# Wide gate-weight splits on VectorE, squares of the last norms in PSUM, and output additions held behind the splits

## The chip, the cores and the metric

The kernel runs on one core of a Trainium2 chip. The metric is the device time of one execution in microseconds (us). The core's engines work side by side, each through a queue of its own in order: TensorE (PE: matmuls, and PEld: weight loads), VectorE (DVE), ScalarE (ACT), GpSimd (POOL), and SyncE (SP), which issues most DMAs. One instruction that waits holds up all that stands behind it on its engine.

## The reference, cut to what matters

One layer of a streaming encoder: token mixers, a gated MLP, then a gated per-layer input. The change touches its end, from the MLP's last down-projection on:

```python
f = (gelu(f_gate) * f_val) @ w_ffn_down        # 2816 -> 1024
h = h + rmsnorm(f, g_ffn_post)                  # second residual
e = p @ w_ple_proj
g = sigmoid(h @ w_ple_gate)                     # the gate, 1024 -> 1024
h = h + rmsnorm(e * g, g_ple_post)              # output
```

There are 1024 tokens and 1024 features, all in float32.

## The kernel before

Activations are held transposed: a tile is 128 features by 1024 tokens, and the work goes in two halves of 512 tokens (half 0 and half 1). A float32 matmul is made of three in a rounded format: each operand is split into `hi`, a rounded copy, and `lo`, the rest, and `linear` adds hi·hi, lo·hi and hi·lo into one PSUM bank. `split` is therefore everywhere: ACT writes `hi` with a CAST (L182), then DVE or POOL writes `lo = src - hi` (L183).

SBUF is cut into 51 slots of 128x1024, PSUM is one tile of eight 128x512 banks. The Python code gives data dependencies; the order of the instructions on each engine is made by a scheduler with a timeline of its own, which may move an instruction far ahead of its place in the code. `tc.issue_after(x)` keeps what it wraps behind the instruction x.

The end of the kernel is written as follows. `down_tail(fX, h)` makes the last six of 22 slices of the down-projection: for each of eight output tiles 18 matmuls, then on DVE `y += psum` (in `down`, L953; half 1 only). `second_residual(h)` squares the eight tiles of y on ACT (`square_sum`, L250), adds the squares up on DVE (L253), and calls `rstd`: matmuls with ones (L230), a short chain on DVE and ACT (L234 to L240, the root on ACT needs a table load), and transposes that spread the result over a PSUM bank (L242). Then for each of eight tiles k: y times the norm (L1037, DVE, reads PSUM), h = d_h1 + y (L1038; POOL for odd k, DVE for even k; `d_h1` is loaded into one of four half slots, so that the loads for k = 4 to 7 wait for the splits of k = 0 to 3), and the split of h (cast on ACT, `lo` on DVE for odd k, on POOL for even k).

The gate follows: `load_all` loads the eight 512 KB weight tiles and splits each in two blocks of 512 columns (`block`: cast on ACT, `lo` on POOL). The loop runs over three pieces (half 0; half 1 in two pieces of 256 tokens). For each of eight tiles of a piece: 24 matmuls (L217), the sigmoid on ACT (L1060, another table than the root's), times e on DVE (L1061), and the square (L250) and its addition (L253). Then `rstd`, and per tile k `hi + lo` on POOL (L1068, it gives h back), the norm on DVE (L1069), their sum (L1070) and the DMA to `out` (L1071).

The squares of these last norms lie in SBUF slots: `sqs` and `sqs2` are rings of half tiles.

Of the kernel before, what the change touches and what calls it, by code (L numbers as in the profile page):

```python
# [28 lines left out]
NBLK = 7  # L29
# [48 lines left out]
def kernel(  # L78
# [19 lines left out]
    nc = tc.nc  # L98
    V, G, A = nc.vector, nc.gpsimd, nc.scalar
# [14 lines left out]
    def slot(i, dt):  # L114
        b, j = quad_of.get(i, (i, None))
        if held[b][0] != dt:
            n = S if j is None else 4 * S
            held[b] = (dt, apool.tile([P, n], dt, tag=f"s{b}", name=f"s{b}"))
        t = held[b][1]
        return t if j is None else t[:, j * S : (j + 1) * S]  # L120
# [8 lines left out]
    def f32(i):  # L129
        return slot(i, F32)  # L130

    def f32r(i):
        return slot(i, F32R)

    def hs(h):
        return slice(h * HALF, (h + 1) * HALF)

    def single(i, h):
        return f32(i)[:, hs(h)]

    def singles(*slots):

        return [(i, h) for i in slots for h in range(2)]
# [5 lines left out]
    def f(ap):  # L149
        return ap.bitcast(F32)  # L150

    def bank(i, n=1):
        return psum[:, i * HALF : (i + n) * HALF]
# [7 lines left out]
    def col(name, i=0):  # L161
        c = COL[name] + i
        return vecs[:, c : c + 1]
# [14 lines left out]
    wblk = Ring(range(NBLK))  # L178
    last = []

    def split(src, hi, lo, eng=None):
        A.copy(hi, src)  # L182
        last.append((eng or V).tensor_sub(lo, src, f(hi)))  # L183
        return last[-1]

    def block(src, eng=None, dst=None):

        n = src.shape[1]
        hi, lo = parts(wblk() if dst is None else dst)
        split(src, hi[:, :n], lo[:, :n], eng or G)  # L190
        return hi, lo

    def wide(src, eng):

        hi, lo = f32r(wblk()), f32r(wblk())
        split(src, hi, lo, eng)
        return [(hi[:, hs(i)], lo[:, hs(i)]) for i in range(2)]

    def load_w(src, raws, cols=1024, dst=(None, None), eng=None):

        raw = f32(raws())
        nc.sync.dma_start(raw[:, :cols], src)
        return [block(raw[:, c : min(c + HALF, cols)], eng, d) for c, d in zip(range(0, cols, HALF), dst)]

    def load_all(w, raws, others):

        where = [None] * NBLK + list(others)
        return [load_w(w[c], raws, dst=where[2 * c : 2 * c + 2]) for c in range(8)]

    def linear(out_ps, w, wc, X, half, cs=None, start=True, stop=True):  # L210

# [33 lines left out]
    def square_sum(acc, src, accs, sqs):  # L245

        n = src.shape[1]
        at = (accs if acc is None else sqs)()
        sq = (single(*at) if isinstance(at, tuple) else bank(at))[:, :n]
        A.activation(sq, src, AF.Square)  # L250
        if acc is None:
            return sq
        V.tensor_add(acc, acc, sq)  # L253
        return acc
# [129 lines left out]
    raws = Ring([7, 8, 42, 43])  # L384
    mm = Ring(range(6))
# [39 lines left out]
    sqs, accs = Ring(singles(44)), Ring(singles(45))  # L425
    es = Ring(range(29, 33))
    B, first, second, third = x_blocks(u, [*range(9, 33), *range(38, 42)])
    for h in range(2):
        acc = None
        for k in range(8):  # L430
            acc = square_sum(acc, single(u[k], h), accs, sqs)
# [36 lines left out]
    w = gate_weights(spilled, True)  # L468
    third(w)
    others = Ring([44, 46])  # L470
# [84 lines left out]
    for grp, dim, pairs in (("kv", 256, ((3, 4),)), ("q", 384, ((0, 1), (2, 5)))):  # L555
        acc = [None, None]
# [33 lines left out]
    raws = Ring([7, 8])  # L590
# [105 lines left out]
    for k in (3, 4):  # L696
# [3 lines left out]
    extra = {  # L700
        2: lambda: [latent(k, "q", "g_q_lat", k) for k in range(3)],
        4: rotary_key,
        13: lambda: key(0, 0, mm),
        14: lambda: [query(0, h, mm) for h in range(2)],
    }
# [25 lines left out]
    sbk, tpb, pob = Ring(range(4)), Ring([4, 5, 6]), Ring([7])  # L731
# [98 lines left out]
    mm = Ring(range(4))  # L830
    mg = Ring(range(42, 51))
    for ft in range(8):
        if ft % 2 == 0:
            w = load_w(w_bout[ft // 2], raws)
# [15 lines left out]
    sqs, accs, accs2 = Ring([5, 6]), Ring(singles(47)), Ring(singles(49))  # L850
    xrs = Ring(singles(42, 43))
    sbk, rbk = Ring([4]), Ring([7])
    B, first, second, third = x_blocks(u, [*range(9, 33), *range(38, 42)])
    for h in range(2):
        acc = None
        for ft in range(8):
# [3 lines left out]
            acc = square_sum(acc, pt, accs, sqs)  # L860
        R = rstd(acc, D, sbk(), rbk())
        acc = None
        for k in range(8):
# [6 lines left out]
            acc = square_sum(acc, y, accs2, sqs)  # L870
# [24 lines left out]
    raws = Ring([42, 43, 7, 8])  # L895
    mm = Ring(range(4))
# [4 lines left out]
    w = up_weights(order[0])  # L901
# [30 lines left out]
    extra = [i for i in free if i not in quad_of][:2]  # L932
    free = [i for i in free if i not in extra]
    yacc = [*free[:6], *before[1:]]
    extra = [42, 43, *extra]
# [55 lines left out]
    mm = Ring(range(6))  # L991
    ends = {}
    for g in range(2):
# [3 lines left out]
        raws = Ring([7, 8] if g else [7, 8, 45, 50])  # L997
# [7 lines left out]
        w = down_weights(0)  # L1005
# [3 lines left out]
        raws = Ring([10, 11, 7, 8] if g else [45, 50, 7, 8])  # L1009
        for i in range(4):  # L1010
            if i:
                w = down_weights(i)
# [7 lines left out]


    hrs = Ring(singles(12, 9))
    sqs, sqs2, accs = Ring(singles(extra[2])), Ring(singles(extra[3])), Ring(singles(50))
    hX = [[None, None] for _ in range(8)]
    hslots = [*range(29, 33), *range(13, 17)], range(17, 25)
    SS, RB = 6, 7

    def second_residual(h):
        acc = None
        for k in range(8):  # L1030
            acc = square_sum(acc, single(yacc[k], h), accs, sqs)
        R = rstd(acc, D, SS, RB)
        for k in range(8):
            hr = single(*hrs())
            nc.sync.dma_start(hr, d_h1[k, :, hs(h)])
            y = single(yacc[k], h)
            V.scalar_tensor_tensor(y, y, col("g_ffn_post", k), R, op0=ALU.mult, op1=ALU.mult)  # L1037
            (G if k % 2 else V).tensor_add(hr, hr, y)  # L1038
            hX[k][h] = parts(hslots[h][k])
            split(hr, *hX[k][h], V if k % 2 else G)  # L1040

    second_residual(0)
    down_tail(fX, 1)
    second_residual(1)

    mm = Ring(range(4))
    sbk, rbk = Ring([4, 5, 6]), Ring([7])
    ers, ors = Ring(singles(10, 11)), Ring(singles(42, 12, 9, 7, 8))
    wgs = load_all(w_gate, raws, [*range(25, 29), 43, *range(38, 42)])
    for h, o, n in ((0, 0, 512), (1, 0, 256), (1, 256, 256)):  # L1050
        acc = None
        cs = slice(o, o + n)
        base = h * HALF + o
        for ft in range(8):
            er = single(*ers())[:, :n]
            nc.sync.dma_start(er, d_e[ft, :, base : base + n])
            pt = bank(mm())[:, :n]
            linear(pt, wgs[ft], 0, hX, h, cs)
            g_ = single(yacc[ft], h)[:, cs]
            A.activation(g_, pt, AF.Sigmoid)  # L1060
            V.tensor_mul(g_, g_, er)  # L1061
            acc = square_sum(acc, g_, accs, sqs2)
        R = rstd(acc, D, sbk(), rbk(), n)
        for k in range(8):
            o_ = single(*ors())[:, :n]
            g_ = single(yacc[k], h)[:, cs]
            hi, lo = hX[k][h]
            G.tensor_add(o_, f(hi[:, cs]), f(lo[:, cs]))  # L1068
            V.scalar_tensor_tensor(g_, g_, col("g_ple_post", k), R, op0=ALU.mult, op1=ALU.mult)  # L1069
            (G if k in (0, 2, 4) else V).tensor_add(o_, o_, g_)  # L1070
            (nc.sync if k % 2 else A).dma_start(out[k * P : (k + 1) * P, base : base + n], o_)  # L1071
# [101 lines left out]
```

## Time and profile before

| | us |
|---|---|
| median of 3 runs | 1529.71 |
| lowest and highest of them | 1528.55, 1529.9 |
| the profiled execution's time | 1530.54 |
| its span, first to last instruction | 1528.7 |
| PE busy | 1472.8 (96%) |
| DVE busy | 1179.2 (77%) |
| ACT busy | 698.6 (46%) |
| POOL busy | 524.0 (34%) |
| mean granted TensorE clock | 0.987 |

PE is busy nearly throughout, so what can be won lies in its few idle stretches and in the stretches in which its clock was granted at half. A timeline row gives the start and the busy time of a run of like instructions on one engine, and in brackets how long the engine was idle before the row and what ended that. A windows row gives the busy time and, in parentheses, the instructions of each engine in one stretch, with the granted clock (PEclk, 1.00 is full speed).

### The profile page before, as it was taken

To read this page: it belongs to the slowest core of one execution; us is meant where nothing else is said; L and a number is where in the kernel's file an instruction comes from. 1 tells how busy PE (TensorE), PEld (TensorE's weight loads), DVE (VectorE), ACT (ScalarE), POOL (GpSimd) and SP (SyncE) were. 2 spreads that over 40 slices of the span, in tenths; PEclk is the share of its full clock that TensorE was granted. 3 is DMA by queue.
4 is the path that set the end of the run, shared out by engine and by line. 5 is a ranking of instruction groups with operands and counts; after the bars stand their busy time and mean duration, and the time that the engine had idled before them with its cause. 6 is when DMAs were issued, how large, how long until landed. Compare 5 with 4: busy or idle time off the path is not lost. (4 is left out here: it accounts for less than half of the span.)

```text
span 1528.7 us, 19246 instructions
## 1 busy us (share of the span) xinstructions
PE 1472.8 (96%) x6980; PEld 1226.6 (80%) x6980; DVE 1179.2 (77%) x1649; ACT 698.6 (46%) x1096; POOL 524.0 (34%) x388
## 2 busy tenths in 40 slices
PE   8989999999989999999997999999999999999896
PEld 6768888888768888888886888888888888787796
DVE  6898566665658888752668888999888889978886
ACT  8634222335447777443454434443434634334333
POOL 1424222215533443441127233344221021333953
PEclk9999999999999999999998999999999999999898
DMA  9325221335761012541380323433334552333432
GB/s 342 129 101 200 90 83 56 124 111 188 261 188 40 27 56 84 193 138 51 121 305 28 104 95 120 129 124 110 112 120 165 186 175 69 124 118 110 138 104 97
DMA packets 73503, 195.56 MB, mean 128 GB/s; under 512 B 7360, under 2 KB 22208, under 8 KB 73408
## 3 DMA queue, kind: packets, MB, share of 16 engines
q1 hardware_dynamic: 65056, 169.90, 34.2%
q10 hardware_dynamic: 8352, 24.44, 4.2%
q8 instruction: 55, 0.90, 0.3%
q14 instruction: 40, 0.33, 0.1%
HBM read 142.79 MB, written 51.51 MB: 127 GB/s over the span
## 5 line engine op out<-in xcount | busy, mean ns | idle before, releaser
L306 PE MATMUL psum<-s,s 128*128 128x512 f32 x3948 | 907.4, 391 | 18.5 <-DVE s L183 14.2
L306 PEld LDWEIGHTS psum<-s,s 128*128 128x128 f32 x3948 | 742.3, 189 | 178.3 <-DVE s L183 17.7
L182 ACT CAST s<-s 128x1024 fp32r<-128x1024 f32 (+3 forms) x419 | 337.3, 828 | 400.5 <-PE psum L306 137.9
L217 PE MATMUL psum<-s,s 128*128 128x512 f32 (+1 forms) x1920 | 416.6, 375 | 17.2 <-ACT s L182 11.5
L183 POOL TENSOR_TENSOR s<-s,s 128x512 fp32r<-128x512 f32 (+2 forms) x150 | 225.8, 1517 | 544.8 <-PE psum L306 352.5
L217 PEld LDWEIGHTS psum<-s,s 128*128 128x128 f32 x1920 | 336.5, 191 | 81.3 <-ACT s L182 14.0
L183 DVE TENSOR_TENSOR s<-s,s 128x1024 fp32r<-128x1024 f32 (+2 forms) x269 | 327.9, 1238 | 52.9 <-ACT s L182 43.2
L535 DVE SCALAR_TENSOR_TENSOR psum<-s,vecs,psum 128x1023 f32<-128x1023 f32 x88 | 111.7, 1279 | 2.5 <-ACT psum L533 1.5
L533 ACT ACTIVATE psum<-s,vecs 128x1024 f32<-128x1024 f32 x44 | 53.2, 1209 | 101.9 <-DVE s L377 88.1
L183 DVE TENSOR_TENSOR s<-psum,s 128x512 fp32r<-128x512 f32 (+3 forms) x144 | 70.8, 504 | 26.9 <-ACT s L182 25.8
L364 POOL TENSOR_TENSOR s<-s 128x512 f32<-128x512 f32 x22 | 33.5, 1523 | 158.1 <-DVE s L322 72.8
L182 ACT CAST s<-psum 128x512 fp32r<-128x512 f32 (+3 forms) x144 | 61.2, 445 | 38.5 <-DVE s L183 13.9
L753 PE MATMUL psum<-s,s 128*128 128x512 f32 (+2 forms) x288 | 67.4, 360 | 2.3 <-ACT s L764 2.1
L250 ACT ACTIVATE s<-s 128x512 f32<-128x512 f32 (+1 forms) x68 | 38.9, 581 | 63.5 <-DVE s L1061 29.9
L766 POOL TENSOR_SCALAR s<-s,ri 128x384 f32<-128x384 f32 (+5 forms) x48 | 41.4, 864 | 70.2 <-DVE ri L765 55.5
L337 POOL TENSOR_TENSOR s<-s,s 128x512 f32<-128x512 f32 x39 | 56.8, 1456 | 2.9
L253 DVE TENSOR_TENSOR s<-s,s 128x512 f32<-128x512 f32 (+1 forms) x55 | 46.0, 837 | 15.2 <-ACT s L250 13.6
L375 DVE TENSOR_TENSOR s<-s,psum 128x512 f32<-128x512 f32 x47 | 32.1, 682 | 31.5 <-PE psum L306 31.4
L336 POOL TENSOR_TENSOR s<-s 128x512 f32<-128x512 f32 x39 | 54.9, 1408 | 2.9
L778 PE MATMUL psum<-s,s 128*128 128x256 f32 x320 | 54.1, 292 | 1.5 <-DVE s L183 0.7
L753 PEld LDWEIGHTS psum<-s,s 128*128 128x128 f32 x288 | 46.4, 189 | 9.9 <-ACT s L764 5.3
L764 ACT ACTIVATE s<-psum,nm 128x128 f32<-128x128 f32 (+3 forms) x64 | 47.6, 746 | 14.3 <-DVE nm L762 9.0
(120 smaller groups left out, 1159.3 us busy)
## 6 DMA issues: line engine op xcount, KB each, us to landing
s<-in_w_up_dram SPq DMA_DIRECT2D x56, 512.0 KB, 3.7
s<-in_w_in_dram SPq DMA_DIRECT2D x40, 512.0 KB, 4.2
s<-in_w_down_dram SPq DMA_DIRECT2D x36, 512.0 KB, 3.7
d_f<-s SPq DMA_DIRECT2D x22, 512.0 KB, 2.6
s<-in_x_dram SPq DMA_DIRECT2D x32, 256.0 KB, 5.4
d_sg<-s ACTq DMA_DIRECT2D x16, 512.0 KB, 3.1
s<-d_sg SPq DMA_DIRECT2D x16, 512.0 KB, 4.3
s<-d_f SPq DMA_DIRECT2D x16, 512.0 KB, 6.7
```

Of the source, the lines that this page charges most:

```text
L182: A.copy(hi, src)
L183: last.append((eng or V).tensor_sub(lo, src, f(hi)))
L217: nc.tensor.matmul(out_ps, w[c // HALF][pw][:, c % HALF : c % HALF + P], X[k][half][px][:, cs], start=start and a == 0 and k == 0, stop=st ...
L253: V.tensor_add(acc, acc, sq)
L306: nc.tensor.matmul(pt, w[pw][:, k * P : (k + 1) * P], blk[k][px], start=a == 0 and k == 0, stop=a == 2 and k == 3,)
L336: who[2].tensor_add(a22, a21, a22)
L337: who[3].tensor_sub(a21, a11, a21)
L533: A.activation(dst, src, AF.Identity, bias=bias, scale=w2)
L535: V.scalar_tensor_tensor(dst[:, i:], src[:, : S - i], w, dst[:, i:], op0=ALU.mult, op1=ALU.add)
L753: nc.tensor.matmul(st_[:, lo_ : lo_ + w_], q[part_q][:, o : o + P], parts(K[hd, kh])[part_k][:, 0:w_], start=part_q == 0 and part_k == 0, ...
L764: A.activation(pr[:, 0:n], st_[:, 0:n], AF.Exp, bias=nm, accum_out=sm)
L778: nc.tensor.matmul(po[:, 0:256], vt[:, kt, :], t_[:, kk * 256 : (kk + 1) * 256], start=kt == 0 and part == 0, stop=kt == 2 * b + 1 and par ...
```

## The change

Three edits, all in the last part of the program:

1. The gate weights go through the new `wide_all`: per weight tile one cast and one `lo` of 128x1024, the `lo` on DVE, in place of two casts and two `lo` of 128x512, the `lo` on POOL. The loads and the slots are the same.
2. The squares of `second_residual` go to PSUM banks 6 and 7, those of the gate norms to banks 4 and 5. L253 then adds a PSUM operand to the SBUF sum. `rstd` of the gate norms keeps one bank, 6, for its sums in place of 4, 5 and 6.
3. Each output addition on POOL (L1068) is kept behind POOL's last split of h of the same half (k = 6).

```diff
-    def wide(src, eng):
-        hi, lo = f32r(wblk()), f32r(wblk())
+    def wide(src, eng, at=(None, None)):
+        hi, lo = (f32r(wblk() if i is None else i) for i in at)
         split(src, hi, lo, eng)
...
+    def wide_all(w, raws, others):
+        where, ws = [None] * NBLK + list(others), []
+        for c in range(8):
+            raw = f32(raws())
+            nc.sync.dma_start(raw, w[c])
+            ws.append(wide(raw, V, where[2 * c : 2 * c + 2]))
+        return ws
...
-    sqs, sqs2, accs = Ring(singles(extra[2])), Ring(singles(extra[3])), Ring(singles(50))
+    sqs, accs = Ring([6, 7]), Ring(singles(50))
+    h_ends = {}
...
-            split(hr, *hX[k][h], V if k % 2 else G)
+            end = split(hr, *hX[k][h], V if k % 2 else G)
+            if k == 6:
+                h_ends[h] = end.ins
...
-    mm = Ring(range(4))
-    sbk, rbk = Ring([4, 5, 6]), Ring([7])
+    mm, sqs = Ring(range(4)), Ring([4, 5])
+    sbk, rbk = Ring([6]), Ring([7])
...
-    wgs = load_all(w_gate, raws, [*range(25, 29), 43, *range(38, 42)])
+    wgs = wide_all(w_gate, raws, [*range(25, 29), 43, *range(38, 42)])
...
-            acc = square_sum(acc, g_, accs, sqs2)
+            acc = square_sum(acc, g_, accs, sqs)
...
-            G.tensor_add(o_, f(hi[:, cs]), f(lo[:, cs]))
+            with tc.issue_after(h_ends[h]):
+                G.tensor_add(o_, f(hi[:, cs]), f(lo[:, cs]))
```

Lines behind the edits have new numbers: L953 becomes L962, L250 and L253 become L259 and L262, L230 and L242 become L239 and L251, L1037 and L1038 become L1047 and L1048, L1060, L1061 and L1068 become L1072, L1073 and L1081. Up to some 200 us from the end all engines have the order of before; then the scheduler's order differs.

DVE where the second half's last down-projection sums stand, before (s_8652 is the sum of squares, s_9629 a square, s_9124 the half slots of h, the others tiles of y; s_4966 is output tile 7):

```order
L953 TENSOR_TENSOR s_102<-s_102,psum 128x512
L253 TENSOR_TENSOR s_8652<-s_8652,s_9629 128x512
L1038 TENSOR_TENSOR s_9124<-s_9124,s_4926 128x512
L253 TENSOR_TENSOR s_8652<-s_8652,s_9629 128x512 x2
L1038 TENSOR_TENSOR s_9124<-s_9124,s_5002 128x512
L953 TENSOR_TENSOR s_4966<-s_4966,psum 128x512
L253 TENSOR_TENSOR s_8652<-s_8652,s_9629 128x512
```

The same place after (s_89 and s_88 hold loaded gate weights):

```order
L962 TENSOR_TENSOR s_5002<-s_5002,psum 128x512
L262 TENSOR_TENSOR s_8652<-s_8652,psum 128x512
L183 TENSOR_TENSOR s_564<-s_89,s_4885 128x1024
L962 TENSOR_TENSOR s_4966<-s_4966,psum 128x512
L262 TENSOR_TENSOR s_8652<-s_8652,psum 128x512
L962 TENSOR_TENSOR s_4926<-s_4926,psum 128x512
L1048 TENSOR_TENSOR s_9124<-s_9124,s_4926 128x512
L183 TENSOR_TENSOR s_188<-s_9124,s_188 128x512
L1048 TENSOR_TENSOR s_9124<-s_9124,s_5002 128x512
L262 TENSOR_TENSOR s_8652<-s_8652,psum 128x512
L183 TENSOR_TENSOR s_389<-s_88,s_137 128x1024
```

The sum for output tile 7 (s_4966) stood behind three additions of squares and two of h; now one addition of a square and one wide gate split stand between it and the sum before it, and seven more wide splits follow.

POOL in the second residual of half 1, before (s_539 and s_119 are h tiles 0 to 3 and 4 to 7 of half 1; from L1068 on rows write output tiles):

```order
L1038 TENSOR_TENSOR s_9124<-s_9124,s_102 128x512
L183 TENSOR_TENSOR s_564<-s_9124,s_564 128x512 x2
L1038 TENSOR_TENSOR s_9124<-s_9124,s_5889 128x512
L1068 TENSOR_TENSOR s_88<-s_188 128x512 x2
L183 TENSOR_TENSOR s_539<-s_9124,s_539 128x512 x2
L1068 TENSOR_TENSOR s_89<-s_539 128x256
L1038 TENSOR_TENSOR s_9124<-s_9124,s_102 128x512
L1038 TENSOR_TENSOR s_9124<-s_9124,s_4966 128x512
L1068 TENSOR_TENSOR s_89<-s_539 128x256
L183 TENSOR_TENSOR s_119<-s_9124,s_119 128x512
L1068 TENSOR_TENSOR s_9124<-s_8807 128x512
L183 TENSOR_TENSOR s_119<-s_9124,s_119 128x512
```

And after:

```order
L1048 TENSOR_TENSOR s_9124<-s_9124,s_102 128x512
L1048 TENSOR_TENSOR s_9124<-s_9124,s_5889 128x512
L183 TENSOR_TENSOR s_539<-s_9124,s_539 128x512 x2
L1048 TENSOR_TENSOR s_9124<-s_9124,s_102 128x512
L1048 TENSOR_TENSOR s_9124<-s_9124,s_4966 128x512
L183 TENSOR_TENSOR s_119<-s_9124,s_119 128x512
L1081 TENSOR_TENSOR s_9124<-s_8807 128x512
L183 TENSOR_TENSOR s_119<-s_9124,s_119 128x512
```

Two gate-weight splits and four of the five output additions have left this stretch; nothing but the chain of h is left in front of its last split, with one addition of half 0.

ACT at the start of the second group of the down-projection's Strassen products, some 210 us from the end, before (s_539 and s_134 are operands of the first products; the COPY takes a product out of PSUM):

```order
L182 CAST s_9289<-s_9124 128x2x512 x2
L182 CAST s_539<-s_9124 128x512
L182 CAST s_134<-s_89 128x512
L319 COPY s_8652<-psum 128x512
L182 CAST s_539<-s_9124 128x512
```

And after:

```order
L182 CAST s_9289<-s_9124 128x2x512 x2
L182 CAST s_539<-s_9124 128x512
L259 ACTIVATE psum<-s_102 128x512
L182 CAST s_134<-s_89 128x512
L328 COPY s_8652<-psum 128x512
L182 CAST s_539<-s_9124 128x512
```

A square of the second residual now stands there, since its place in PSUM is free early; it waits for POOL's addition that ends its tile of y (L364 in the kernel before).

On PE the two norms of the second residual now lie further apart: between the transposes of half 0 and the ones-matmul of half 1 stand 147 matmuls of 128x512, where 90 stood. Behind the transposes of half 1 stand 86 of them up to half 1's first gate matmul, where 143 stood. On ACT, two more table loads stand in half 0 (sigmoid, root, sigmoid again), since one gate tile's sigmoid comes before the root of half 1.

## Rows read from the trace of the kernel before

**Rows 1.** Timeline of PE: start, busy, line, shape, count, idle before and releaser

```profile
1375.82 4.49 PE L217 MATMUL psum<-s,s 128*128 128x512 f32 x16
1381.45 6.44 PE L217 MATMUL psum<-s,s 128*128 128x512 f32 x27 [1.14 <-DVE s L183]
...
1395.70 0.60 PE L242 MATMUL psum<-ident,rs_r 128*128 128x128 f32 x4
1396.06 18.87 PE L217 MATMUL psum<-s,s 128*128 128x512 f32 x82
...
1420.16 2.50 PE L217 MATMUL psum<-s,s 128*128 128x512 f32 x5 [4.00 <-DVE s L953]
...
1433.72 0.60 PE L242 MATMUL psum<-ident,rs_r 128*128 128x128 f32 x4
1434.08 38.20 PE L217 MATMUL psum<-s,s 128*128 128x512 f32 x189
1472.95 1.05 PE L230 MATMUL psum<-ones,s 128*128 128x1 f32 x8 [0.67 <-DVE s L253]
```

**Rows 2.** Windows of 2 us: busy (instructions) of PE, PEld, DVE, ACT, POOL, then PEclk

```profile
1420.00:1422.00 2.00, 1.84 (x4) 1.49 (x5) 1.24 (x2) 1.29 (x3) 2.00 (x3) 0.50 0.00 0
...
1428.00:1430.00 2.00, 2.00 (x6) 1.52 (x6) 1.44 (x2) 0.50 (x1) 2.00 (x3) 0.50 0.89 215
```

**Rows 3.** Timeline of DVE in front of the wait of 4.00 us

```profile
1411.12 1.67 DVE L253 TENSOR_TENSOR s<-s,s 128x512 f32<-128x512 f32 x1
...
1414.41 3.43 DVE L253 TENSOR_TENSOR s<-s,s 128x512 f32<-128x512 f32 x2
1417.76 1.75 DVE L1038 TENSOR_TENSOR s<-s,s 128x512 f32<-128x512 f32 x1
1419.43 0.68 DVE L953 TENSOR_TENSOR s<-s,psum 128x512 f32<-128x512 f32 x1
```

**Rows 4.** Groups by line and shape from 1355 us on: busy, mean ns, idle before

```profile
L217 PE MATMUL psum<-s,s 128*128 128x512 f32 x336 | 82.8, 406 | 5.5 <-DVE s L953 4.0 <-DVE s L183 1.1 <-ACT s L182 0.3
L183 POOL TENSOR_TENSOR s<-s,s 128x512 fp32r<-128x512 f32 x24 | 35.3, 1494 | 28.2 <-PE psum L217 16.0 <-ACT s L182 12.2
L253 DVE TENSOR_TENSOR s<-s,s 128x512 f32<-128x512 f32 x21 | 23.6, 1124 | 5.2 <-ACT s L250 4.5
L183 DVE TENSOR_TENSOR s<-s,s 128x1024 fp32r<-128x1024 f32 x7 | 8.3, 1213 | 0.0
```

**Rows 5.** Groups by line and shape over the whole span: L253 with a PSUM operand

```profile
L253 DVE TENSOR_TENSOR s<-s,psum 128x512 f32<-128x512 f32 x28 | 19.1, 686 | 39.6 <-ACT psum L250 39.0
```

**Rows 6.** Timeline around 1335 us: a wide split on DVE while POOL works

```profile
1334.57 5.63 POOL L371 TENSOR_TENSOR s<-s,s 128x512 f32<-128x512 f32 x3 [11.22 <-DVE s L365]
...
1336.73 2.31 DVE L183 TENSOR_TENSOR s<-s,s 128x1024 fp32r<-128x1024 f32 x1
```

**Rows 7.** Timeline of POOL in the second residual of half 1

```profile
1423.50 14.73 POOL L183 TENSOR_TENSOR s<-s,s 128x512 fp32r<-128x512 f32 x11
...
1439.44 2.99 POOL L183 TENSOR_TENSOR s<-s,s 128x512 fp32r<-128x512 f32 x2
...
1444.10 3.00 POOL L1068 TENSOR_TENSOR s<-s 128x512 f32<-128x512 f32 x2
...
1461.87 1.67 POOL L1068 TENSOR_TENSOR s<-s 128x512 f32<-128x512 f32 x1 [0.63 <-DVE s L183]
1463.51 1.73 POOL L183 TENSOR_TENSOR s<-s,s 128x512 fp32r<-128x512 f32 x1
```

**Rows 8.** Timeline of ACT: a cast near 1318 us, and a table load

```profile
1317.87 0.62 ACT L182 CAST s<-s 128x512 fp32r<-128x512 f32 x1 [1.46 <-DMA s<-in_w_down_dram]
...
1473.70 1.28 ACT L235 ACT_TABLE_LOAD   x1
```

**Rows 9.** Timeline of PE: the wait behind that cast

```profile
1323.36 2.12 PE L306 MATMUL psum<-s,s 128*128 128x512 f32 x8 [1.71 <-ACT s L182]
```

**Rows 10.** The window of 4 us that holds it, columns as in rows 2

```profile
1322.00:1326.00 4.00, 2.30 (x9) 1.61 (x10) 3.93 (x5) 2.62 (x3) 1.35 (x1) 1.00 0.01 5
```

## Prediction

> **What bounds the kernel now.** I read the page's busy shares first (the table): PE is busy for 96% of the span, so only its waits and its half-speed stretches can give time back. The timeline of PE over the changed end of the program comes next [rows 1]. The reader is to see there a stretch from 1375.82, where half 1's down-projection tail begins, to half 1's gate, in which PE does nothing but matmuls of 128x512 and two norms. How much of it is lost? 336 such matmuls lie behind 1355 us [rows 4], and one takes 18.87 / 82 = 0.230 us undisturbed [rows 1], so 77.3 us of work. A norm costs PE about 1.2 us (its transposes 1396.06 - 1395.70 = 0.36; its ones-matmuls 1.05 less the overlap of their end, about 0.8), two of them 2.4. Of the 336, 193 stand in rows ahead of 1434.08 (the 34 of two rows not shown among them), so 143 follow, and half 1's gate begins at 1434.08 + 143 x 0.230 = 1467.0. Elapsed are 91.2 us, work is 79.7, and 11.5 us are lost.
>
> Three items hold it. PE waits 1.14 for a split and 4.00 for a sum of L953 [rows 1]. After the 4.00 the granted clock stands at 0.50, first row 1420, last 1428, five windows of 2 us, in which PE begins about six matmuls where the full clock allows eight or nine [rows 2]: 1.2 GHz in place of 2.4, so 5.0 us. The remaining 1.4 is in pieces too small for a row here.
>
> Why 4.00? The timeline of DVE in front of it [rows 3] shows the sum ready to go but queued: from 1411.12 to 1419.43 DVE spends 8.3 us on three additions of squares and two of h, one of which first waits for its load. Additions of squares from two SBUF operands average 1124 ns here [rows 4] and 1.67 to 1.72 in this queue [rows 3]. With a PSUM operand the same addition has a mean of 686 ns over 28 [rows 5]. POOL is what differs: it works without pause here, with gate splits above all, 24 splits and 35.3 us behind 1355 [rows 4].
>
> **The change, part by part.**
>
> *Squares in PSUM.* Fourteen additions of the second residual go from a mean of 1.12 to about 0.69, 6 us less of DVE; no one waits for most of it, and what it is worth is inside the wait of 4.00. ACT's squares cost it the same instruction. In the new order the sum of output tile 7 stands behind one such addition and one wide split, 0.69 + 1.21 to 2.31 [rows 4 to 6], where 8.3 us stood; PE comes to the gate 72 matmuls or 16.6 us after half 0's transposes. So the 4.00 goes, and the 5.0 of clock with it.
>
> The order has a cost far ahead: one square is hoisted in front of a cast that began at 1317.87 [rows 8], on whose successors PE waited 1.71 [rows 9]. The square waits for an addition of POOL that ended about 1 us later, so the cast begins about 1.5 later. PE there has slack in the other operands: between 0 and 1.5, and I take 0.5, since the cast nearest PE's wait was itself held by a load. The clock stayed at 1.00 across that wait [rows 10], so I charge none.
>
> *Wide splits on DVE.* POOL loses 16 splits of 1.49, 23.9 us [rows 4]. DVE gains eight at 1.21 free [rows 4] or 2.31 beside POOL [rows 6]. They lie between the end of half 0's eight norm products and half 1's ones-matmul. PE has 147 matmuls there, 33.8 us, less about 5.4 for the norm products: 28.4 us for DVE. Its queue holds 11 operations with PSUM at 0.60 from start to start, nine wide splits at 1.13 and eight of 512 at 0.60 (estimates from the durations in [rows 3 to 5], less their overlap): 21.6 us if nothing contends. If every operation with two SBUF operands takes its price beside POOL (2.31 and 1.7), 41.0. POOL has 12 operations of about 1.5 there, 18 us, so it is busy 63% of the time; at that share, the operations on SBUF run at 0.65 of their free speed, and DVE needs 6.6 + 15.0 / 0.65 = 29.7. That is 1.3 late. ACT's queue has the like: the cast of h tile 6 stands behind the cast of the last gate weight, which waits for its load, and by my walk along the queues PE waits 1.3 for it. These two waits overlap in part; I take 2.0 together, bounds 0 and 12.6 (all contended). Single waits of this size did not lower the clock [rows 10].
>
> The Trainium skill, "GPSIMD Engine Reference", section "8. Key points", says that POOL shares its SBUF interfaces with VectorE and contends with VectorE's instructions that have two SBUF inputs. The rows agree (2.31 against 1.21, and 686 ns where one operand is in PSUM). Taken alone this speaks for the second edit and against the first: wide splits keep two SBUF inputs. With all of them contended it would give the third rival below.
>
> *Table loads.* ACT loads two more tables in half 0, 1.28 each [rows 8]. One lies in the chain of half 1's norm, which 31 matmuls or 7.1 us cover; the rest of that chain takes nearly that. Bounds 0 and 2.6; I take 0.3. The Trainium skill, "ScalarE: Activation LUTs", section "What ACT_TABLE_LOAD costs", gives some 2.66 us with a drain for each switch; by that figure the two would be 5.3, and my term at most 3 us more. The load's row here has 1.28.
>
> *Output additions behind the splits.* They move POOL's order in the second residual of half 1, which decides the next wait. Before, the transposes end the norm at 1433.72 and POOL's last split of h ends at 1463.51 + 1.73 = 1465.24 [rows 1, 7]: 31.5 us. PE had 143 matmuls or 33 us over it. Now it has 86, 19.8 us, and 22 of half the width (about 0.12 each) until that split is needed: 22.7 us with the transposes. What shortens the chain: POOL's 11 gate splits end at 1438.23, about 2.5 after its first addition could have begun; two more gate splits, 2.99; five output additions between 1444.10 and 1461.87, about 7 (3.00 for two, 1.67 for the last, about 1.2 for each of two half as wide), of which one of 1.6 stays. 31.5 - 2.5 - 3.0 - 5.4 = 20.6 if all lay on the chain; my walk along the queues, with h loads and casts, gives 22.4. The margin is 0.3 to 2, so no stall is charged; the bounds are 0 and 8.8 (31.5 against 22.7).
>
> *The rest.* The wait of 1.14 at 1381.45 stands behind additions that get shorter: between 0 and 1.14, and I take 0.6. The 1.4 of small pieces I leave at 1.1. The wait of 0.67 for the gate's squares [rows 1] may go; nothing is booked. The tail behind 1473 keeps its order.
>
> **The sum.** Against the profiled execution's 1530.54: -11.5, then +0.5 (hoisted square), +2.0, +0.3, +0.6, +1.1 = 4.5 kept or new, net -7.0: 1523.5. That execution was 0.8 above the median, so **1522.5** in runs like the three shown. The forecast's own range is 1519.5 to 1526.
>
> **The rivals.**
>
> 1. *Nothing slips.* All of the 11.5 and the 0.67 go: 1530.5 - 12.2 - 0.8 = 1517.5. For it: the walk's waits are short. Against: each rests on a queue that is nearly full.
> 2. *A new wait takes the old one's place.* ACT's casts of h and of gate weights now stand in one queue behind loads; if PE idles 4 us in half 0's gate as it did before, the clock falls again for 5 us: 1523.5 - 2.0 + 9.0 - 0.8 = 1529.7, no change. For it: a full PE was thrown to 0.50 by just such a wait [rows 2].
> 3. *DVE becomes the bound (slower).* At 41.0 us for 28.4, PE waits 12.6 for the last square of half 1: 10.6 beyond the 2.0 booked, and 5 of clock: 1522.7 + 15.6 = 1538. It makes the kernel measurably slower from about 5 us beyond my term, so from 35 us of DVE, that is if some 70% of the operations on SBUF contend where I count 42%. For it: DVE's queue in [rows 3] is contended throughout; against: POOL loses half its work there.
> 4. *Half 1's chain stays long (slower).* At 31.5 PE waits 8.8, and 5 of clock follows: 1522.7 + 13.8 = 1536.5. It turns slower from a chain of 28 us. Against: 11 us of what POOL did there is gone.
>
> That the change does little of what it says (the sum of tile 7 leaves its queue but the additions stay slow) would end like rival 2.
>
> **How the numbers follow.** Chances: the forecast 0.62, nothing slips 0.09, a new wait 0.17, DVE the bound 0.06, the long chain 0.06. The range 1517.5 to 1530 holds the forecast, half of the first rival and most of the second: 0.8. Within 0.2%, or 3.06 us, a measurement of this kernel can't tell from none; so faster means below 1526.65 and slower above 1532.77. Faster: 0.62 + 0.09 and a mild form of the new wait, 0.02: 0.73. Same: 0.15. Slower: 0.12.
>
> **What would show it.** Right: no wait of PE above 2 us between 1375 and 1470, PEclk 1.00 throughout it, additions of squares at 0.69, and half 1's gate about 7 us earlier. The wide splits should average between 1.3 and 2.0. Wrong: a window at 0.50 in half 0's gate (rival 2 or 3: the releaser is ACT L182 or DVE L262), a wait above 3 us at half 1's first gate tile (rival 4, releaser POOL or ACT L182), or a wait near 1322 that grew by over 2 us with the clock lowered behind it.

## The result, and the profile after

The changed kernel takes 1520.02 us (median of 4 runs, 1519.08 to 1520.53) against 1529.65 of the kernel before: a ratio of 0.9934, 95% interval 0.9922 to 0.9947, so 9.6 us faster. A second set of runs beside the experiments gave 1518.99 against 1528.28, 0.9938 (0.9924 to 0.9952). The profiled execution has a span of 1517.8 us.

The page's busy line of the kernel after has a little less work on DVE and POOL, and the same matmuls on PE:

```profile
PE 1469.9 (97%) x6980; PEld 1225.4 (81%) x6980; DVE 1163.1 (77%) x1657; ACT 700.0 (46%) x1090; POOL 499.9 (33%) x372
```

The timeline of PE over the changed end (start, busy, line, shape, count, idle before and releaser), to lay beside [rows 1] and [rows 9]:

```profile
1319.13 3.02 PE L315 MATMUL psum<-s,s 128*128 128x512 f32 x12 [1.09 <-ACT s L182]
1322.86 2.11 PE L315 MATMUL psum<-s,s 128*128 128x512 f32 x8 [0.71 <-ACT s L182]
1325.32 50.18 PE L315 MATMUL psum<-s,s 128*128 128x512 f32 x220 [0.35 <-DVE s L183]
1375.35 10.62 PE L226 MATMUL psum<-s,s 128*128 128x512 f32 x46
...
1392.65 0.60 PE L251 MATMUL psum<-ident,rs_r 128*128 128x128 f32 x4
1393.00 19.32 PE L226 MATMUL psum<-s,s 128*128 128x512 f32 x84
1412.77 14.70 PE L226 MATMUL psum<-s,s 128*128 128x512 f32 x63 [0.45 <-ACT s L182]
1427.31 0.95 PE L239 MATMUL psum<-ones,s 128*128 128x1 f32 x8
...
1435.29 0.60 PE L251 MATMUL psum<-ident,rs_r 128*128 128x128 f32 x4
1435.64 20.48 PE L226 MATMUL psum<-s,s 128*128 128x512 f32 x92
1456.33 5.06 PE L226 MATMUL psum<-s,s 128*128 128x256 f32 x40 [0.21 <-ACT s L182]
1462.00 1.05 PE L239 MATMUL psum<-ones,s 128*128 128x1 f32 x8 [0.61 <-DVE s L262]
```

The waits of 1.14 and 4.00 are gone; 0.45, 0.21 and 0.61 are what is left between 1375 and 1462. Half 1's gate begins at about 1435.64 + 86 x 0.229 = 1455.3, 80.0 us after 1375.35, where the count of work was 79.7. The last norms' ones-matmul comes at 1462.00 instead of 1472.95; behind it the two kernels take the same time to the end (55.8 us each).

Two windows over the half clock of [rows 2] (busy of PE, PEld, DVE, ACT, POOL, then PEclk, the granted clock) show 1.00 throughout:

```profile
1420.00:1440.00 20.00, 20.00 (x95) 16.67 (x95) 14.69 (x24) 11.74 (x16) 4.66 (x4) 1.00 0.42 141
1440.00:1460.00 20.00, 19.79 (x104) 16.93 (x104) 15.00 (x20) 8.80 (x15) 15.43 (x12) 1.00 0.24 73
```

The groups by line and shape from 1355 us on (busy, mean ns, idle before), against [rows 4]:

```profile
L226 PE MATMUL psum<-s,s 128*128 128x512 f32 x336 | 77.9, 391 | 0.4 <-ACT s L182 0.4
L183 DVE TENSOR_TENSOR s<-s,s 128x1024 fp32r<-128x1024 f32 x15 | 20.7, 1390 | 0.0
L183 POOL TENSOR_TENSOR s<-s,s 128x512 fp32r<-128x512 f32 x8 | 14.8, 1860 | 10.7 <-ACT s L182 10.7
L262 DVE TENSOR_TENSOR s<-s,psum 128x512 f32<-128x512 f32 x21 | 14.3, 683 | 3.2 <-ACT psum L259 2.0 <-ACT s L259 0.8
```

The 21 additions of squares went from a mean of 1124 to 683 ns. Seven of the 15 wide splits stood there before; the eight of the gate weights, from 1404 to 1428 us, average 1542 ns, between the free 1.21 us and 2.31:

```profile
L183 DVE TENSOR_TENSOR s<-s,s 128x1024 fp32r<-128x1024 f32 x8 | 12.2, 1542 | 0.0
```

POOL has 8 splits left of 24, but each takes 1.86 us in place of 1.49. Both engines slow here while both work on SBUF operands.

### The profile page after: what moved, and what is told of

It is laid out like the page before. It is cut to its first block, busy times and chain, and to the rows that moved or that the text cites. A ratio compares the mean times of both kernels' runs of the same rounds, so it can differ in the third digit from the quotient of the medians.

```text
span 1517.8 us, 19230 instructions
## 1 busy us (share of the span) xinstructions
PE 1469.9 (97%) x6980; PEld 1225.4 (81%) x6980; DVE 1163.1 (77%) x1657; ACT 700.0 (46%) x1090; POOL 499.9 (33%) x372
## 5 line engine op out<-in xcount | busy, mean ns | idle before, releaser
L315 PE MATMUL psum<-s,s 128*128 128x512 f32 x3948 | 909.1, 392 | 17.7 <-DVE s L183 13.8
L315 PEld LDWEIGHTS psum<-s,s 128*128 128x128 f32 x3948 | 743.1, 189 | 178.3 <-DVE s L183 17.6
L226 PE MATMUL psum<-s,s 128*128 128x512 f32 (+1 forms) x1920 | 411.6, 372 | 9.4 <-ACT s L182 9.3
L226 PEld LDWEIGHTS psum<-s,s 128*128 128x128 f32 x1920 | 334.3, 190 | 71.3 <-ACT s L182 11.4
L183 DVE TENSOR_TENSOR s<-s,s 128x1024 fp32r<-128x1024 f32 (+2 forms) x277 | 336.9, 1236 | 57.0 <-ACT s L182 48.4
L183 POOL TENSOR_TENSOR s<-s,s 128x512 fp32r<-128x512 f32 (+2 forms) x134 | 205.0, 1540 | 525.0 <-PE psum L315 332.5
L262 DVE TENSOR_TENSOR s<-s,psum 128x512 f32<-128x512 f32 (+1 forms) x63 | 39.3, 625 | 46.1 <-ACT psum L259 44.0
L345 POOL TENSOR_TENSOR s<-s 128x512 f32<-128x512 f32 x39 | 54.8, 1404 | 2.9
L762 PEld LDWEIGHTS psum<-s,s 128*128 128x128 f32 x288 | 46.4, 189 | 9.9 <-ACT s L773 5.3
L787 PEld LDWEIGHTS psum<-s,s 128*128 128x128 f32 x320 | 45.4, 189 | 6.0 <-DVE s L183 2.0
```

Source lines behind the costliest of these rows:

```text
L226: nc.tensor.matmul(out_ps, w[c // HALF][pw][:, c % HALF : c % HALF + P], X[k][half][px][:, cs], start=start and a == 0 and k == 0, stop=st ...
L315: nc.tensor.matmul(pt, w[pw][:, k * P : (k + 1) * P], blk[k][px], start=a == 0 and k == 0, stop=a == 2 and k == 3,)
L345: who[2].tensor_add(a22, a21, a22)
L762: nc.tensor.matmul(st_[:, lo_ : lo_ + w_], q[part_q][:, o : o + P], parts(K[hd, kh])[part_k][:, 0:w_], start=part_q == 0 and part_k == 0, ...
L787: nc.tensor.matmul(po[:, 0:256], vt[:, kt, :], t_[:, kk * 256 : (kk + 1) * 256], start=kt == 0 and part == 0, stop=kt == 2 * b + 1 and par ...
```

## The experiments

Two figures stand for each kernel. The timed ratio is against the kernel before on the same chip, with its interval. The *end part* is read from the one trace of each kernel: from the start of the 220 matmuls at 1325.32 (or the row that answers to it) to the end of the span. It leaves out the front of the program, where half-clock stretches ahead of 850 us come and go between executions of all these kernels and spread even the kernel before over 1523.9 to 1533.5.

| kernel | edits | ratio (95%) | against before, us | end part, us |
|---|---|---|---|---|
| before | none | 1 | 0 | 202.9 |
| only_wide | 1 | 0.9990 (0.9980 to 1.0000) | -1.4 | 198.7 |
| only_psum | 2 | 0.9981 (0.9972 to 0.9990) | -2.9 | 197.8 |
| only_hold | 3 | 0.9996 (0.9985 to 1.0007) | -0.6 | 201.0 |
| no_hold | 1, 2 | 0.9965 (0.9952 to 0.9979) | -6.5 | 195.4 |
| no_wide | 2, 3 | 0.9970 (0.9959 to 0.9980) | -5.0 | 196.4 |
| no_psum | 1, 3 | 0.9999 (0.9989 to 1.0009) | +0.1 | 201.2 |
| after_again | 1, 2, 3 | 0.9938 (0.9924 to 0.9952) | -9.3 | 191.3 |
| wide_pool | 1 on POOL, 2, 3 | 0.9974 (0.9963 to 0.9984) | -3.9 | 196.7 |
| narrow_dve | 1 in halves (and w_o's splits), 2, 3 | 0.9972 (0.9962 to 0.9982) | -4.6 | 195.5 |
| psum_h | 1, half of 2, 3 | 0.9979 (0.9970 to 0.9987) | -3.4 | 197.2 |
| psum_gate | 1, other half of 2, 3 | 0.9969 (0.9958 to 0.9980) | -5.4 | 195.7 |
| late16 | 1, 2, 3 and a longer chain | 1.0017 (1.0006 to 1.0027) | +2.3 | 203.1 |

The end parts put all twelve some 1 to 3 us further below before than the timed medians do. One cause would explain them all: the one trace of before had an end part about 2 us above its usual. That is inferred, since before was traced once. Two traces of the changed kernel differ by 1.2 us in their end parts (192.5 for the one shown above, 191.3 for after_again), so a difference of that size says nothing.

The half clock in these end parts, up to 1480 us, costs about 5 us in before and late16, 3.4 in only_wide, only_psum and psum_h, 1.7 in only_hold, no_hold, no_wide, no_psum, wide_pool and narrow_dve, and nothing in psum_gate and the changed kernel (added up from PEclk in windows of 2 us).

Times in the expectations were set against 1529.7 us for before and 1520.0 for the changed kernel. Beside the experiments these two took about 1528.1 and 1519.0, so the expectations are read as differences.

**One edit alone.** Edit 1 alone, as a difference from the changed kernel (edit 2 taken back, edit 3 too):

```diff
-    sqs, accs = Ring([6, 7]), Ring(singles(50))
+    sqs, sqs2, accs = Ring(singles(extra[2])), Ring(singles(extra[3])), Ring(singles(50))
...
-    mm, sqs = Ring(range(4)), Ring([4, 5])
-    sbk, rbk = Ring([6]), Ring([7])
+    mm = Ring(range(4))
+    sbk, rbk = Ring([4, 5, 6]), Ring([7])
...
-            acc = square_sum(acc, g_, accs, sqs)
+            acc = square_sum(acc, g_, accs, sqs2)
...
-            with tc.issue_after(h_ends[h]):
-                G.tensor_add(o_, f(hi[:, cs]), f(lo[:, cs]))
+            G.tensor_add(o_, f(hi[:, cs]), f(lo[:, cs]))
```

> Edit 1 alone: gate weights split wide on VectorE; squares stay in SBUF, output additions free. Theory A (POOL's gate splits slowed VectorE's additions with two SBUF operands, and that made the wait of 4.00 us with its 5 us of half clock): with 16 splits off POOL the squares' additions fall from 1.12 to about 0.8 us, no PE wait above 2 us, 1521 to 1524 us. Theory B (VectorE's queue is simply too long, and eight wide splits make it longer; it takes the PSUM squares to pay for them): the squares stay above 1.0 us, a PE wait of 2 to 6 us stays, 1527 to 1533 us.

1526.75 us. Theory B is nearer: the squares still take 0.98 us, and a wait of 2.99 stays, with a clock of 0.50 from 1416 to 1420. The timeline of DVE in front of it shows why:

```profile
1409.00 4.55 DVE L183 TENSOR_TENSOR s<-s,s 128x1024 fp32r<-128x1024 f32 x2
1413.47 1.75 DVE L262 TENSOR_TENSOR s<-s,s 128x512 f32<-128x512 f32 x1
1415.14 0.67 DVE L962 TENSOR_TENSOR s<-s,psum 128x512 f32<-128x512 f32 x1
```

Two wide splits at 2.3 and a square at 1.75, all at their price beside POOL, stand where the squares stood. Less POOL work alone doesn't free the sum of tile 7.

Edit 2 alone (gate weights by the old call; the additions are free again, as in the diff above):

```diff
-    wgs = wide_all(w_gate, raws, [*range(25, 29), 43, *range(38, 42)])
+    wgs = load_all(w_gate, raws, [*range(25, 29), 43, *range(38, 42)])
...
```

> Edit 2 alone: squares in PSUM; gate weights split in halves on POOL as before. Theory A: the additions take 0.69 us beside a busy POOL, the sum of output tile 7 leaves its queue in time, no half clock: 1521 to 1524 us. Theory C (the gain comes from POOL's chain: its gate splits stand in front of h's splits): POOL still holds h of half 0 back, a PE wait of 2 to 4 us and half clock stay: 1526 to 1530 us.

1525.2 us. The squares take 682 ns beside a POOL that is as busy as before (24 splits, 33.7 us): with one operand in PSUM they cost no more there, as theory A has it. But waits of 1.11 and 1.00 on casts of h and of 0.99 on a sum of L962 remain, and two stretches of 0.50 behind them, so the time is nearer to theory C's. That POOL's gate splits are what holds h back is argued from POOL's queue. Neither theory has it whole.

Edit 3 alone:

> Edit 3 alone: output additions held behind POOL's splits. Theory A: VectorE's queue in front of the sum of output tile 7 is the same, so the wait of about 4 us and the half clock stay: 1528 to 1530.5 us. Theory C (POOL's chain is what counts): 1522 to 1526 us.

1527.56 us, no change within the interval, as theory A has it. The wait has another releaser, a cast on ACT, with 2.91 in place of 4.00, and the clock did not fall behind it. It fell later, to 0.50 at 1470, behind a wait of 2.20 for the last square of half 0's gate. PE's row and the window after it (columns as above):

```profile
1416.53 3.25 PE L226 MATMUL psum<-s,s 128*128 128x512 f32 x13 [2.91 <-ACT s L182]
```

```profile
1418.00:1420.00 2.00, 1.78 (x8) 1.13 (x6) 2.00 (x2) 0.87 (x3) 2.00 (x3) 1.00 0.66 227
```

**All but one.** Without edit 3:

> The changed kernel without edit 3. Theory A: the output additions fill POOL's free time in any case, 1520 to 1522 us, within 0.15% of the changed kernel. Theory C: half 1's chain of h grows by up to 5 us of additions and PE waits for it at half 1's first gate tile: 1523 to 1528 us.

1521.61 us, 2.8 less of a gain than the whole (-6.5 against -9.3; the intervals 0.9952 to 0.9979 and 0.9924 to 0.9952 touch at one end). That lies just under theory C's 3 to 8 and above theory A's 2.3; theory C's place is wrong. Half 1's chain is no longer than in the changed kernel, and PE doesn't wait there. It waits in half 0, 2.63 for a cast of h, with a clock of 0.50 and 0.72 in the next two windows. The timeline of PE, then that of POOL ahead of it:

```profile
1415.33 13.48 PE L226 MATMUL psum<-s,s 128*128 128x512 f32 x51 [2.63 <-ACT s L182]
```

```profile
1402.32 2.36 POOL L1080 TENSOR_TENSOR s<-s 128x512 f32<-128x512 f32 x1
1404.65 1.29 POOL L183 TENSOR_TENSOR s<-s,s 128x512 fp32r<-128x512 f32 x1
1405.90 1.74 POOL L1080 TENSOR_TENSOR s<-s 128x512 f32<-128x512 f32 x1
1407.61 4.51 POOL L1048 TENSOR_TENSOR s<-s,s 128x512 f32<-128x512 f32 x2
```

Two output additions, 2.36 and 1.74, stand in front of the additions that make h's tiles 5 and 7. These end 21.8 us after half 0's transposes (1390.31 to 1412.12), in the changed kernel 17.4 us after them (1392.65 to 1410.06), since the same rows there are:

```profile
1402.67 4.35 POOL L183 TENSOR_TENSOR s<-s,s 128x512 fp32r<-128x512 f32 x2 [3.93 <-ACT s L182]
1406.98 3.08 POOL L1048 TENSOR_TENSOR s<-s,s 128x512 f32<-128x512 f32 x2
```

Without edit 1:

> The changed kernel without edit 1 (gate weights in halves on POOL, with the squares in PSUM and the additions held). If edit 1 and the two others are worth separate waits (their sum from the runs of one edit each, counted from the last Strassen pair to the end: 4.2, 5.1 and 2.0 us): 5 to 7 us faster than before, 3 to 5 slower than the changed kernel; PE waits on casts of h of 1 to 3 us in half 0's gate with some half clock. If POOL's splits only matter through VectorE's additions of squares, which are safe in PSUM: within 1.5 us of the changed kernel.

1523.28 us, 4.3 less of a gain: the first reading. The waits are 0.52, 1.16 (ACT's cast) and 2.21, and a window of 0.50 follows the last. With the squares in PSUM a sum of L962 is late once more:

```profile
1417.14 4.58 PE L226 MATMUL psum<-s,s 128*128 128x512 f32 x12 [2.21 <-DVE s L962]
```

In front of that sum VectorE has two additions of h at 1.62 and 1.16 and a split at 1.76, all of two SBUF operands, while POOL works on splits of 512 columns from 1411.19 to 1417.52.

Without edit 2:

> The changed kernel without edit 2 (squares in SBUF, wide splits on VectorE, additions held). VectorE's queue now holds the wide splits and additions with two SBUF operands in front of the sum of output tile 7: a PE wait of 2 to 5 us on it and half clock behind, 3 to 6 us slower than the changed kernel. If the wide splits alone are the cure (POOL free, so nothing contends): within 1.5 us of it.

1528.39 us: no gain at all, a loss of 9.4 against the whole, more than the 3 to 6 expected. The wait of 4.00 has indeed gone (0.92 is left). Others came. The timeline of PE:

```profile
1416.53 11.42 PE L226 MATMUL psum<-s,s 128*128 128x512 f32 x49 [0.92 <-ACT s L182]
...
1436.85 0.65 PE L251 MATMUL psum<-ident,rs_r 128*128 128x128 f32 x4 [1.69 <-DVE rs_r L249]
...
1463.38 3.14 PE L226 MATMUL psum<-s,s 128*128 128x256 f32 x24 [1.01 <-POOL s L183]
1469.15 1.05 PE L239 MATMUL psum<-ones,s 128*128 128x1 f32 x8 [2.62 <-DVE s L262]
1470.06 6.04 PE L226 MATMUL psum<-s,s 128*128 128x256 f32 x36
```

VectorE is late at half 1's norm and at the last square of half 0's gate, and POOL at a split of half 1's h; behind the 2.62 the 36 matmuls take 6.04 in place of 4.55. At the norm a load has a part in it: a product with e (L1073) that stands in front of the norm's operations waits 1.76 us for its load. This is the mechanism of the prediction's third rival, in the kernel that keeps two-operand squares, but not at the place it named: PE didn't wait for half 1's last square.

**Which squares.** The gate's squares back in SBUF, and then those of the second residual:

```diff
# psum_h
-            acc = square_sum(acc, g_, accs, sqs)
+            acc = square_sum(acc, g_, accs, sqs2)
...
# psum_gate
-    sqs, accs = Ring([6, 7]), Ring(singles(50))
+    sqs, accs = Ring(singles(extra[2])), Ring(singles(50))
```

> The changed kernel with the gate norms' squares back in SBUF; only those of the second residual stay in PSUM. If the squares of the second residual are the ones that matter (they stand in VectorE's queue between the sums, the wide splits and h): within 2 us of the changed kernel. If the gate's matter too, through half 1's chain: 3 us or more slower, with a PE wait at the last norms' ones-matmul.

> The changed kernel with the second residual's squares back in SBUF; only the gate's in PSUM. First reading: 6 to 10 us slower than the changed kernel, at the time of the kernel before, as without edit 2 altogether. Second reading (the waits of that run at the last norms came from the gate's squares): 3 to 5 us slower.

Both halves matter. psum_h loses 5.9 against the whole (-3.4 against -9.3). Nearly all of it falls at one place, the last square of half 0's gate: the wait below, and 36 matmuls behind it that take 7.18 in place of 4.55. PE's row, DVE's last squares in front of it, and a window behind it:

```profile
1464.03 1.46 PE L239 MATMUL psum<-ones,s 128*128 128x1 f32 x8 [2.61 <-DVE s L262]
```

```profile
1457.00 1.77 DVE L1073 TENSOR_TENSOR s<-s,s 128x512 f32<-128x512 f32 x1
1459.47 1.00 DVE L262 TENSOR_TENSOR s<-s,s 128x512 f32<-128x512 f32 x1 [0.70 <-ACT s L259]
1460.40 1.22 DVE L1073 TENSOR_TENSOR s<-s,s 128x512 f32<-128x512 f32 x1
1462.32 1.66 DVE L262 TENSOR_TENSOR s<-s,s 128x512 f32<-128x512 f32 x1 [0.70 <-ACT s L259]
```

```profile
1466.00:1468.00 2.00, 2.00 (x11) 2.00 (x11) 0.34 (x2) 1.97 (x3) 0.00 (x0) 0.50 0.19 66
```

psum_gate loses 3.9: the second reading by its size. Its waits are 1.14, 0.92 and 1.66 (the last at half 1's norm), without the 2.62.

**Width and engine of the gate splits.**

```diff
# wide_pool
-            ws.append(wide(raw, V, where[2 * c : 2 * c + 2]))
+            ws.append(wide(raw, G, where[2 * c : 2 * c + 2]))
# narrow_dve: load_all for the gate, its lo on VectorE (load_all splits w_o too)
-        return [load_w(w[c], raws, dst=where[2 * c : 2 * c + 2]) for c in range(8)]
+        return [load_w(w[c], raws, dst=where[2 * c : 2 * c + 2], eng=V) for c in range(8)]
```

> The changed kernel with the eight wide lo splits on POOL in place of VectorE: width without the change of engine. If the engine matters (POOL's queue holds h's splits, and POOL takes about 2.6 to 3 us for each wide split): half 0's gate waits 2 to 6 us for h or for weights, 4 to 9 us slower than the changed kernel. If the width matters (half as many casts and splits to issue): within 2 us of it.

> The changed kernel with the gate weights split in halves of 512 columns, but on VectorE: the change of engine without the width. 16 splits at 0.68 to 1.7 us in place of eight at 1.21 to 2.31: 0.15 to 1 us more for a pair. If the engine is what matters: within 2 us of the changed kernel. If the width matters too (VectorE was near its limit): 3 to 6 us slower.

wide_pool is 5.4 behind the whole: the engine matters, at 2768 ns for each wide split on POOL. Its wait of 2.59 on a cast of h, half clock behind, is of the kind that no_hold has; another of 1.64 follows at half 1's norm.

narrow_dve is 4.7 behind (its trace is of the fastest of its eight runs). PE waits 1.93 at half 1's norm, and the clock falls to 0.50 for a window after that. PE's row, and VectorE ahead of it:

```profile
1435.42 0.80 PE L251 MATMUL psum<-ident,rs_r 128*128 128x128 f32 x4 [1.93 <-DVE rs_r L249]
```

```profile
1434.01 0.69 DVE L1073 TENSOR_TENSOR s<-s,s 128x512 f32<-128x512 f32 x1 [1.73 <-ACT s L1072]
1434.61 0.15 DVE L246 TENSOR_TENSOR rs_t<-rs_r 128x4 f32<-128x4 f32 x1
```

The 16 half splits are not what is late there; the last of them ended at 1425.61. The norm's operations stand behind a product with e, the product waits for ACT's sigmoid, and the sigmoid stood behind a table load that ran from 1432.08 to 1433.36. So half of the gain is lost with the width, but by way of another order of the queues; that the smaller number of splits is itself worth something isn't shown. The edit reaches further than the gate, too: `load_all` also splits the output projection's weights (w_o, near 650 us), and those 16 splits go to VectorE as well. So the timed 4.7 isn't the gate's alone; the end part, which leaves that out, is 4.2 us longer than after_again's.

**The margin of half 1's chain.** Sixteen multiplications by one in tile 7 of half 1:

```diff
+            for _ in range(16 if h and k == 7 else 0):
+                V.tensor_scalar(y, y, 1.0, 0.0, op0=ALU.mult, op1=ALU.add)
             (G if k % 2 else V).tensor_add(hr, hr, y)
```

> The changed kernel with 16 multiplications by one on VectorE in half 1's tile 7, between its norm and its addition: they lengthen half 1's chain of h by some 5 to 8 us and leave all else. With the margin of the prediction (0.3 to 2 us) PE waits 3 to 7 us at half 1's first gate tile, and if a wait of that size lowers the clock, 2 to 5 us go at half speed behind it: 5 to 11 us slower than the changed kernel. If the chain has slack of 5 us or more: within 2 us of it.

1530.27 us, 11.6 more than the changed kernel by the differences to before. The multiplications took 10.8 us (0.41 to 0.43 for the shortest, up to 1.5 beside POOL). PE's waits, then VectorE ahead of the longest:

```profile
1459.55 2.06 PE L226 MATMUL psum<-s,s 128*128 128x256 f32 x15 [0.69 <-ACT s L182]
1463.16 1.09 PE L226 MATMUL psum<-s,s 128*128 128x256 f32 x7 [1.55 <-ACT s L1074]
1469.89 1.87 PE L239 MATMUL psum<-ones,s 128*128 128x1 f32 x8 [5.64 <-DVE s L262]
```

```profile
1464.21 3.67 DVE L1049 TENSOR_SCALAR s<-s 128x512 f32<-128x512 f32 x7
1467.80 0.69 DVE L1075 TENSOR_TENSOR s<-s,s 128x512 f32<-128x512 f32 x1
1469.15 0.69 DVE L262 TENSOR_TENSOR s<-s,psum 128x512 f32<-128x512 f32 x1 [0.33 <-ACT psum L259]
```

The waits sum to 7.9, 7.1 more than in the changed kernel from half 1's gate on; most of the rest is half clock behind them, at 0.50 from 1466 to 1474. But this does not measure the margin of half 1's chain. At half 1's first gate tile PE waits only 0.69, not the 3 to 7 expected. The 5.64 is for the last square of half 0's gate: the product with e that it squares (L1075 here) stands behind seven of the multiplications in VectorE's queue. PE's order is another too: the ones-matmul of half 0's gate stands behind 28 of half 1's gate matmuls, where 46 stood. The lengthened chain was late at the same time (the cast of h's tile 7 ended at 1470.81). So the third rival's mechanism and the fourth's come out together here, and together they make the kernel 0.17% slower than before; what each would cost alone was not separated. The margin can be read from the changed kernel: PE waits 0.21 there for a cast of h, and not at all in after_again, so at that cast it is about nothing.

## Why the prediction was right, point by point

Sign and range held: 1520.0 where 1522.5 was forecast, in 1517.5 to 1530, 2.5 us beyond the forecast on the good side and within its own 1519.5 to 1526. (By its own sum the forecast is 1522.7, not 1522.5: 1523.5 less 0.8. In [rows 1] the rows not shown hold 63 of the 193 matmuls, not 34; the 193 is right.) Part of the closeness is luck. What was kept or new was put at 4.5 us and was about 1 in the trace, and the 11.5 to be won was probably some 2 too much for before's usual runs; the two errors go against each other.

- *What is lost now: 11.5 us.* The rows bear the reading out: 80.0 us elapse after, with 79.7 of work. But the trace read was probably about 2 us above before's usual in its end part, as the twelve comparisons suggest, so a timed gain of 11.5 was not to be had. The first rival, nothing slips, nearly came true in the trace: 11.2 of the 11.5 went, the 0.67 became 0.61, and the end part as a whole fell by 10.4. The timed gain of 9.3 to 9.6 lies between that rival and the forecast.
- *The wait of 4.00 and its half clock.* Right in cause, while the cure takes more than the prediction gave it. Squares and additions of two SBUF operands beside POOL filled the queue; in PSUM the squares take 683 ns, and in the changed kernel the sum of tile 7 goes through. But PSUM squares without the wide splits leave a wait for a sum of L962, 0.99 in only_psum and 2.21 in no_wide, and wide splits alone leave 2.99; edits 1 and 3 together remove it without PSUM squares (no_psum, where 0.92 is left for a cast). What only PSUM squares do is keep VectorE from being late further on.
- *Wide splits on VectorE, term +2.0.* Mis-sized: 0.45 was paid. VectorE's last square of half 1 ended at 1425.64 and PE wanted it at 1427.31, 1.7 us early where 1.3 late was booked. Two steps of the estimate failed. It counts nine wide splits in front of that square, but the ninth stands behind it; that is 1.7 us at the prediction's price. And it lets the operations on SBUF run at 0.65 of their free speed. The 16 in front of the square took about 18 us from start to start where 13.8 would be free, so about 0.76 (an estimate from their durations). POOL was not less busy than the 63% booked (18.0 us from 1400 to 1425.6), but only 5 of the 16 were lengthened; POOL paid as well, 1.86 for a split that took 1.28 at its shortest. The Trainium skill, "GPSIMD Engine Reference", section "8. Key points", was drawn on for contention of VectorE's two-SBUF-input operations with POOL; the runs agree, and they show that the delay falls on POOL as well.
- *Table loads, term +0.3.* Nothing was paid: PE reached half 1's transposes at 1435.29 without a wait. Between the load and the root lie 0.02 us in the rows below (ACT), so the larger figure with a drain, cited from "ScalarE: Activation LUTs" of the Trainium skill, section "What ACT_TABLE_LOAD costs", isn't seen in this trace. In narrow_dve a table load does hold the norm, by the order of the queues there.

```profile
1429.54 1.28 ACT L244 ACT_TABLE_LOAD   x1
1430.84 0.20 ACT L244 ACTIVATE rs_t<-rs_v 128x4 f32<-128x4 f32 x1
```

- *Hoisted square, term +0.5.* The waits there are 1.09 + 0.71 + 0.35 = 2.15 where before has 1.71 + 0.34 = 2.05: 0.1.
- *The rest, terms +0.6 and +1.1.* The wait of 1.14 at 1381.45 has gone whole. It goes with the second residual's squares: 1.14 or 0.75 is left in the kernels that keep them in SBUF (only_hold, no_psum, psum_gate, only_wide), 0 to 0.65 in those that have them in PSUM. Of the 1.1 in small pieces nothing is seen: 80.0 us elapse up to half 1's gate, for 79.7 of work.
- *Output additions behind the splits.* The step that failed in kind. The prediction gave them 5.4 us in half 1's chain and nothing at PE. The chain did fall to 22.4 us (1435.29 to 1457.64), the walk's figure, but it is 22.3 without the hold (no_hold, 1436.18 to 1458.44) and 31.0 with the hold and POOL's gate splits (no_wide, 1428.61 to 1459.58). Edit 1 alone makes most of the shortening (only_wide, 1437.59 to 1462.02: 24.4), edit 2 the rest, and the hold none. What the hold saves is a wait of 2.63 and its half clock in half 0's gate, 2.8 us by the timed runs; the prediction did not look at POOL's order in half 0.
- *The second rival* did not come in the changed kernel, but in five of the experiments: in half 0's gate PE waits 2.91, 2.63 and 2.59 for a cast (only_hold, no_hold, wide_pool) and 2.99 and 2.21 for a sum (only_wide, no_wide). The kernel stands close to it on several sides at once. That fits edits worth 1.4, 2.9 and 0.6 alone making 9.3 together: each removes waits that the others leave standing, and of the experiments of part of the change only psum_gate has no half clock left behind such waits.

That no_psum ends at the time of before while its 4.00 wait is gone is shown by its rows. The edits also make the scheduler choose another order: the hoisted square, for one, is there only in the kernels with the second residual's squares in PSUM. How much of each gain or loss that order alone makes was not separated from the cost of the operations; a run with the order kept and only the place of the squares changed would be needed.

## What to carry to other kernels

When an engine's operations slow beside another's, look at the second operand: a partial result that only one addition reads can lie in PSUM. That addition took 682 to 686 ns here whether POOL worked or not, against a mean of 1124 with both operands in SBUF. Count a queue's time at both prices, and look for who waits behind it, on both engines that contend. Where an engine is near its limit, expect edits to be worth little one by one and much together, so test them by leaving one out as well as by adding one.

## What the runs showed of the hardware that was not expected

- The granted clock fell to 0.50 after waits of 4.00 (before), 2.99 (only_wide), 2.63 (no_hold), 2.62 (no_psum), 2.61 (psum_h), 2.59 (wide_pool), 2.21 (no_wide), 2.20 (only_hold) and 1.93 us (narrow_dve), and in only_psum after waits of 0.99 and 1.00, but stayed at 1.00 after 2.91 (only_hold) and 1.71 ([rows 9, 10]). The length of the one wait doesn't decide it. What does decide was not tried.
- VectorE's tiny operations suffer too. In before, three of the operations of half 1's norm on 128x4 took 1.2 us each while POOL worked, where half 0's took 0.16 with POOL idle; they take 0.16 in the changed kernel with POOL idle, and 2.3 in wide_pool beside POOL's wide splits. From the timeline of DVE, before, then after, then wide_pool:

```profile
1425.28 1.21 DVE L238 TENSOR_TENSOR rs_t<-rs_t,rs_v 128x4 f32<-128x4 f32 x1
...
1428.29 1.19 DVE L240 TENSOR_TENSOR rs_r<-rs_r,rs_t 128x4 f32<-128x4 f32 x1
```

```profile
1388.16 0.16 DVE L247 TENSOR_TENSOR rs_t<-rs_t,rs_v 128x4 f32<-128x4 f32 x1
```

```profile
1427.13 2.31 DVE L247 TENSOR_TENSOR rs_t<-rs_t,rs_v 128x4 f32<-128x4 f32 x1
```
